# The second block's side tasks begin one in four slots instead of four in five

## The chip, the cores and the metric

The kernel runs on one core of one Trainium2 chip, as one program with one launch. The metric is device time in microseconds of one execution. Three executions of the kernel before took 2336.18 us in the median (2334.62 to 2336.28).

The engines are named as in the profile: PE is TensorE (matmuls; PEld its weight loads), DVE is VectorE, ACT is ScalarE, POOL is GpSimd, SP is SyncE, which issues the loads of the weights.

## The reference, cut to what matters

Everything is float32. A two-layer first block (attention, pooling, a Fourier mix; 256 tokens and 256 context tokens, width 2048) gives `x`, and a second block of one layer works on it. The second block's first half is what the change touches:

```
h = rmsnorm(x, norm1_g)
p = h @ w_in                                  # 2048 -> 4096 columns
u, v = split(gelu(p[:, :2048]))               # 1024 columns each
v = layernorm(v);  mixed = tril(ws) applied over 128-token chunks, per head, + bs
y_gm = u * mixed
g, xl = p[:, 2048:3072], p[:, 3072:]
xr = causal convolution of xl over 4 tokens
r, i = sigmoid(xr @ wa + ba), sigmoid(xr @ wx + bx)      # per head
a = exp(-8 * r * softplus(-lam)); b = sqrt(1 - a*a) * i * xr
y_lru = scan(h_t = a_t * h_{t-1} + b_t) * gelu(g)
x = x + concat(rmsnorm(y_gm), rmsnorm(y_lru)) @ w_out
```

After it come the feed-forward half (2048 to 2 x 6144 columns with a convolution of 3 tokens, then back to 2048) and a last rmsnorm.

## The kernel before, in words

**Matmuls.** Features lie on partitions, 128 at a time: `self.h[k]` is the k-th of 16 tiles. To keep float32 precision, each operand is split into a high part (rounded to the PE's format) and a low part (the rest), and each product is three matmuls: high x high, high x low, low x high (`mm3`, L203 to L205). Weights come from memory as 128 x 1024 blocks (`wraw`), are split by ACT (`whi`, L263) and DVE (`wlo`, L264) into one of three buffers each, and are used by 24 matmuls of 256 columns, or 12 of 512. A buffer is free again when its matmuls are done. The weight splits are written with high priority once the kernel's startup is over.

**The second block's projections.** `block2` (L1061) runs four projections of 1024 columns, 16 weight blocks each, which I call P1 to P4 by their order: P1 the recurrence's input (columns 3072 on), evacuated by `lru_front` (L1114); P2 `v`, evacuated by `evac_v` (L1172); P3 the recurrence's gate, evacuated by `lru_out` (L1159); P4 `u`, evacuated by `gm_out` (L1194), which also does the small matmuls that mix `v` (`gm_mix`, L1200). The last two of a projection's 16 blocks are one step, and the evacuations stand in that step. Then all that is waiting is run (`flush`), and the output projection follows, two times 1024 columns, over the order k = 8 to 15 (the recurrence's tiles) and then 0 to 7 (the gm tiles). Its evacuation is `resid2` (L1228).

**The side work.** What is neither a projection nor its evacuation is a task: a Python function put in a queue with `defer` while the program is written. The queue is served in order, first come first served. `spend` (L174) counts the time of the projections' matmuls by a formula of the kernel's own and calls `tick` once per 1.25 us of it. A tick is a slot. It goes on with tasks that have asked to pause for some slots (`yield n`), adds `start_rate` to a credit that is capped at 4, and begins a task for each whole credit while fewer than four are paused. `flush` ticks until queue and paused tasks are empty, without any matmul between. The tasks of P1 to P4, in the order in which they enter the queue:

- `block2_rstd` (L979; pauses 8, then 3 slots): the two norms' scales `r1`, `r12`, which `lru_front` needs
- `begin`: takes the tile for the two sums of squares, `sqm` and `sql`
- at the end of P1, eight `lru_conv` (L1119), then eight `lru_gates` (L1128; pause 2 slots) and eight `lru_scan` (L1152; a Sqrt on ACT, a product on POOL, the scan on DVE)
- at the end of P2, two `layernorm_v` (L1178)
- at the end of P3, eight `lru_gate` (L1165): the product with the gate, its square (`sum_sq`, L872, on ACT) and the sum of squares on POOL; then `norm_branch` for the recurrence (L1213; pauses 6 slots)
- at the end of P4, `norm_branch` for the gm tiles (pauses 0 slots)

`norm_branch` sums over features with a matmul by ones (`ssum`, L503), takes the power -0.5 on POOL (L497), broadcasts it by a matmul (`rbc`, L526), and for each of eight tiles makes the product `yn` (DVE, L1222), its high part (ACT, L263) and its low part (DVE, L264).

**What sets the order on an engine.** The program is written in one order, and the framework's scheduler then lays out each engine's instructions: of those that are ready it takes the one of highest priority, which is the one written first, except that the weight splits go ahead. An engine runs its own list strictly in that order. Short-lived tiles come from rings: `S` (L56) has seven tiles and holds `xl`, `gl`, `gu` (the evacuations), the squares `sqt`, `yn`, `rbn`, `res` and more. `C` (L53) has eight and holds `xr`, `vt` and `ym`.

The lines that make a slot's starts:

```
        self.start_acc = min(self.start_acc + self.start_rate, 4.0)
        while self.start_acc >= 1.0 and self.queue and len(self.active) < 4:
```

Of the kernel before, what the change touches and what calls it, by code (L numbers as in the profile page):

```python
# [32 lines left out]
class Kern:  # L33
# [1027 lines left out]
    def block2(self):  # L1061
        nc, a = self.nc, self.a
        w_in, w_out = a["w_in_2"][0], a["w_out_2"][0]
        ks = list(range(KT))
        hi = lambda k: self.h[k][0][:, 0:256]
        lo = lambda k: self.h[k][1][:, 0:256]
        self.xr, self.yl, self.ym = [None] * 8, [None] * 8, [None] * 8
        self.vt, self.yh, self.h3 = {}, {}, []

        later = lambda fn, *args: ([], partial(self.defer, fn, *args))  # L1070

        def begin():
            sqp = self.E("sqp")
            self.sqm, self.sql = sqp[:, 0:256], sqp[:, 256:512]

        steps = [([], self.flush), later(self.block2_rstd), later(begin), ([], partial(self.rate, 0.8))]
        steps += self.proj_fm(w_in, 3072, 1024, ks, hi, lo, NX, self.lru_front)
        steps += [later(self.lru_gates, i) for i in range(8)] + [later(self.lru_scan, i) for i in range(8)]
        steps += self.proj_tm(w_in, 1024, 1024, ks, hi, lo, 2, self.evac_v)
        steps += [later(self.layernorm_v, t) for t in range(2)]  # L1080
        steps += self.proj_fm(w_in, 2048, 1024, ks, hi, lo, NX, self.lru_out)
        steps.append(later(self.norm_branch, self.yl, "lru_out_g", 8))
        steps += self.proj_fm(w_in, 0, 1024, ks, hi, lo, NX, self.gm_out)
        steps += [later(self.norm_branch, self.ym, "gm_out_g", 0), ([], self.flush)]
        order = list(range(8, 16)) + list(range(8))

        def begin_out():
            self.sq2 = self.E("sq2")[:, 0:256]
            self.x2d = self.dr.tile([NX, D], F32, name="x2d")
        steps.append(([], begin_out))  # L1090

        def evac(g, b, ps):
            for j in range(2):
                self.resid2(g * 8 + b * 2 + j, ps[:, j * 256:(j + 1) * 256])
        for g in range(2):
            steps += self.proj_fm(w_out, g * 1024, 1024, order, lambda k: self.yh[k][0], lambda k: self.yh[k][1], NX,
                                  partial(evac, g))

        def end():
            yield 8  # L1100
            rb = self.rstd_tokens(self.sq2, 2, D)
            self.r3b = self.E("r3b", shape=(P, 256))
            nc.vector.tensor_copy(self.r3b, rb[:, :256])
        steps.append(later(end))
        return steps
# [305 lines left out]
```

## Time and profile before

| | us |
|---|---|
| median of three executions | 2336.18 |
| the profiled execution | 2334.31 |
| its span | 2332.5 |
| PE busy | 2254.2 |
| DVE busy | 1605.9 |
| ACT busy | 1007.1 |
| POOL busy | 205.9 |

Of the span, the second block's P1 to P4 take about 1190 to 1397 us and the output projection about 1397 to 1489 us. The feed-forward half follows to the end. Busy times of different engines overlap, so they don't add up to the span. An engine's idle time is put down to what ended it. A matmul's duration in a row is longer than the distance to the next one, because matmuls are pipelined: with 256 columns they start 0.12 us apart and show 0.28 us.

### The profile page before, as it was taken

Reading aid. Unit: us, or ns where it says so; the run is one execution under the profiler, and the core shown is the slowest. Engines: PE = TensorE matmul, PEld = TensorE weight load, DVE = VectorE, ACT = ScalarE, POOL = GpSimd, SP = SyncE. Lnnn points to the kernel's source line nnn. Section 1 sums busy time; section 2 is a strip of 40 time slices with the busy share of each in tenths; the row PEclk is TensorE's granted clock in tenths of the full one; section 3 lists DMA queues with packets and bytes.
Section 4 is the critical chain, followed back from the end, with each engine's and each line's share of the span. In section 5 each row is a group of like instructions: output and inputs, shape, how many; then the busy total and the mean of one; then the engine's idle time right before and its main releaser. Section 6 shows DMA issues by size and latency. Waiting matters only on the chain. (4 is left out here: it accounts for less than half of the span.)

```text
span 2332.5 us, 37418 instructions
## 1 busy us (share of the span) xinstructions
PE 2254.2 (97%) x14672; PEld 1977.0 (85%) x14672; DVE 1605.9 (69%) x2575; ACT 1007.1 (43%) x1511; POOL 205.9 (9%) x262
## 2 busy tenths in 40 slices
PE   7899999999999999999999999999999999999998
PEld 3567778777778878799998899999999999988886
DVE  3369988799987768655678776656676576564444
ACT  3133443223223554444446554544554455443433
POOL 1011011100112110100221111200000000000100
PEclk9999999999999999999999999999999999999999
DMA  9896545466866556655554555666566665765564
GB/s 316 288 310 209 154 125 152 127 209 209 277 216 212 173 170 208 192 152 183 171 169 156 173 164 167 195 192 186 183 182 183 185 184 182 220 205 189 185 188 142
DMA packets 202720, 447.88 MB, mean 192 GB/s; under 512 B 15848, under 2 KB 60288, under 8 KB 202544
## 3 DMA queue, kind: packets, MB, share of 16 engines
q1 hardware_dynamic: 193088, 428.93, 59.0%
q0 software_dynamic: 3888, 11.18, 1.4%
q10 hardware_dynamic: 5568, 5.40, 0.8%
q8 instruction: 115, 1.88, 0.3%
q14 instruction: 61, 0.50, 0.1%
HBM read 437.05 MB, written 8.39 MB: 191 GB/s over the span
## 5 line engine op out<-in xcount | busy, mean ns | idle before, releaser
L264 DVE TENSOR_TENSOR wlo<-wraw,whi 128x1024 fp32r<-128x1024 f32 x608 | 751.6, 1239 | 541.5 <-ACT whi L263 540.1
L263 ACT CAST whi<-wraw 128x1024 fp32r<-128x1024 f32 x608 | 636.0, 1049 | 925.6 <-PE acc L204 585.8
L203 PE MATMUL acc<-phi,whi 128*128 128x256 f32 (+1 forms) x1600 | 477.1, 298 | 0.9 <-DVE xT L830 0.8
L205 PE MATMUL acc<-phi,wlo 128*128 128x256 f32 (+1 forms) x1600 | 473.7, 296 | 3.5 <-DVE wlo L264 3.5
L204 PE MATMUL acc<-plo,whi 128*128 128x256 f32 (+1 forms) x1600 | 473.7, 296 | 0.0
L203 PE MATMUL acc<-h3t,whi 128*128 128x256 f32 x1536 | 435.2, 283 | 2.0 <-DVE xT L1233 2.0
L204 PE MATMUL acc<-h3t,whi 128*128 128x256 f32 x1536 | 434.8, 283 | 0.0
L205 PE MATMUL acc<-h3t,wlo 128*128 128x256 f32 x1536 | 434.7, 283 | 0.0
L328 DVE SCALAR_TENSOR_TENSOR acc<-wraw,silu_c,acc 128x512 f32<-128x512 f32 x420 | 297.5, 747 | 40.0 <-DMA wraw<-in_ada_w_dram 38.4
L203 PEld LDWEIGHTS acc<-phi,whi 128*128 128x128 f32 x1600 | 302.6, 189 | 13.6 <-issue 3.6
L205 PEld LDWEIGHTS acc<-phi,wlo 128*128 128x128 f32 x1600 | 302.5, 189 | 13.6 <-DVE wlo L264 4.3
L204 PEld LDWEIGHTS acc<-plo,whi 128*128 128x128 f32 x1600 | 302.8, 189 | 9.1 <-issue 0.5
L203 PEld LDWEIGHTS acc<-h3t,whi 128*128 128x128 f32 x1536 | 294.8, 192 | 2.7 <-DVE xT L1233 2.7
L205 PEld LDWEIGHTS acc<-h3t,wlo 128*128 128x128 f32 x1536 | 294.8, 192 | 0.1
L204 PEld LDWEIGHTS acc<-h3t,whi 128*128 128x128 f32 x1536 | 294.8, 192 | 0.0
L203 PE MATMUL acc<-hhi,whi 128*128 128x512 f32 x384 | 159.2, 415 | 1.1 <-ACT whi L263 1.1
L204 PE MATMUL acc<-hlo,whi 128*128 128x512 f32 x384 | 153.4, 400 | 0.0
L205 PE MATMUL acc<-hhi,wlo 128*128 128x512 f32 x384 | 152.0, 398 | 0.2 <-DVE wlo L264 0.2
L204 PE MATMUL acc<-wlo,act 128*128 128x512 f32 x384 | 151.7, 395 | 0.0
L205 PE MATMUL acc<-whi,act 128*128 128x512 f32 x384 | 151.7, 395 | 0.0
L203 PE MATMUL acc<-whi,act 128*128 128x512 f32 x384 | 151.7, 395 | 0.0
L203 PEld LDWEIGHTS acc<-hhi,whi 128*128 128x128 f32 x384 | 72.9, 190 | 22.2 <-issue 4.6
(350 smaller groups left out, 2790.2 us busy)
## 6 DMA issues: line engine op xcount, KB each, us to landing
wraw<-in_w_in_dram SPq DMA_DIRECT2D x216, 512.0 KB, 3.9
wraw<-in_ffn_w_up_dram SPq DMA_DIRECT2D x192, 512.0 KB, 3.6
wraw<-in_ada_w_dram SPq DMA_DIRECT2D x128, 512.0 KB, 4.4
wraw<-in_w_out_dram SPq DMA_DIRECT2D x104, 512.0 KB, 4.2
wraw<-in_ffn_w_down_dram SPq DMA_DIRECT2D x96, 512.0 KB, 3.8
apage<-in_ada_w_dram SPq DMA_DIRECT2D x128, 256.0 KB, 6.0
xd<-xT SPq DMA_DIRECT2D x16, 256.0 KB, 4.7
xT<-xd POOLq DMA_DIRECT2D x16, 256.0 KB, 5.6
```

The costliest lines, as they stand in the source:

```text
L203: mm(out, lhi, rhi, start=start, stop=False)
L204: mm(out, lhi, rlo, start=False, stop=False)
L205: mm(out, llo, rhi, start=False, stop=stop)
L263: self.nc.scalar.copy(hi, src)
L264: self.nc.vector.tensor_tensor(lo, src, f(hi), ALU.subtract)
L328: nc.vector.scalar_tensor_tensor(acc[m], x, cm, acc[m], ALU.mult, ALU.add)
```

## The change

One number: the credit that a slot adds while the second block's projections run is 0.25 instead of 0.8. The next change of the rate, to 0.3 at the beginning of the feed-forward half, stays.

```
-        steps = [([], self.flush), later(self.block2_rstd), later(begin), ([], partial(self.rate, 0.8))]
+        steps = [([], self.flush), later(self.block2_rstd), later(begin), ([], partial(self.rate, 0.25))]
```

## Rows read from the trace of the kernel before

**Rows 1.** The page's first part: busy us, share of the span, instructions.
```profile
PE 2254.2 (97%) x14672; PEld 1977.0 (85%) x14672; DVE 1605.9 (69%) x2575; ACT 1007.1 (43%) x1511; POOL 205.9 (9%) x262
```

**Rows 2.** Stretches P2 and P4: length, busy time by engine, granted clock, DMA share, GB/s.
```profile
1242.60:1299.50 56.90, 53.02 (x227) 41.54 (x226) 56.71 (x78) 42.49 (x61) 15.35 (x15) 1.00 0.44 140
...
1346.00:1397.30 51.30, 50.84 (x429) 50.43 (x428) 35.88 (x57) 27.75 (x43) 10.83 (x11) 1.00 0.52 167
```

**Rows 3.** Waits, 1205 to 1500 us: who for whom, total us, times, longest.
```profile
PE acc L204 <- DVE wlo L264: 3.8, 4, 2.9
...
PE acc L205 <- DVE wlo L264: 1.0, 1, 1.0
```

**Rows 4.** Timeline of DVE: start us, duration, instruction, idle before it.
```profile
1418.06 0.42 DVE L1232 TENSOR_TENSOR res<-xT,rbp 128x256 f32<-128x256 f32 x1
...
1443.16 0.42 DVE L1232 TENSOR_TENSOR res<-xT,rbp 128x256 f32<-128x256 f32 x1
```

**Rows 5.** Timeline of PE, the small matmuls of the norms and P4's end.
```profile
1210.40 0.61 PE L985 MATMUL s<-ones,sq 128*128 128x1 f32 x4 [2.65 <-POOL sq L880]
...
1361.39 0.50 PE L503 MATMUL ssum<-ones,sqp 128*128 128x1 f32 x4
...
1363.26 0.71 PE L526 MATMUL rbc<-bcw,ones 128*128 128x128 f32 x4 [0.43 <-DVE bcw L525]
...
1397.37 0.36 PE L203 MATMUL acc<-phi,whi 128*128 128x256 f32 x1
...
1406.32 0.61 PE L503 MATMUL ssum<-ones,sqp 128*128 128x1 f32 x4 [1.24 <-POOL sqp L880]
...
1408.38 0.68 PE L526 MATMUL rbc<-bcw,ones 128*128 128x128 f32 x4 [0.29 <-DVE bcw L525]
```

**Rows 6.** Timeline of POOL behind P4: the last additions, the power.
```profile
1403.62 0.74 POOL L880 TENSOR_TENSOR sqp<-sqp,sqt 128x256 f32<-128x256 f32 x1 [2.13 <-ACT sqt L879]
1404.88 1.38 POOL L880 TENSOR_TENSOR sqp<-sqp,sqt 128x256 f32<-128x256 f32 x1 [0.51 <-ACT sqt L879]
1407.20 0.71 POOL L497 TENSOR_TENSOR rs_col<-rs_col,nhalf 128x2 f32<-128x2 f32 x1 [0.94 <-DVE rs_col L496]
```

**Rows 7.** Timeline of ACT and DVE in the two norms and between.
```profile
1364.93 0.80 ACT L263 CAST phi<-yn 128x256 fp32r<-128x256 f32 x2 [0.55 <-DVE yn L1222]
...
1401.47 1.23 DVE L264 TENSOR_TENSOR wlo<-wraw,whi 128x1024 fp32r<-128x1024 f32 x1 [0.46 <-ACT whi L263]
...
1409.19 0.36 ACT L1219 COPY rbn<-rbc 128x256 f32<-128x256 f32 x1
```

**Rows 8.** Groups by line of DVE, 1390 to 1421 us: busy, mean ns, idle before.
```profile
L1222 DVE SCALAR_TENSOR_TENSOR yn<-ym,cols,rbn 128x256 f32<-128x256 f32 x8 | 3.5, 482 | 0.0
...
L264 DVE TENSOR_TENSOR plo<-yn,phi 128x256 fp32r<-128x256 f32 x8 | 3.0, 421 | 0.0
```

**Rows 9.** Stretches of 2 us in P1; PE's granted clock is third from the end.
```profile
1212.00:1214.00 2.00, 1.41 (x10) 1.25 (x9) 1.18 (x4) 0.40 (x1) 0.71 (x1) 0.71 0.17 64
1214.00:1216.00 2.00, 2.00 (x11) 2.00 (x11) 1.56 (x6) 0.00 (x0) 0.00 (x1) 0.50 0.28 74
```

**Rows 10.** Groups by line of ACT, 1240 to 1305 us: busy, mean ns, idle before.
```profile
L263 ACT CAST whi<-wraw 128x1024 fp32r<-128x1024 f32 x18 | 18.4, 1042 | 3.9 <-PE acc L205 3.4 <-ACT xr L1123 0.5
L1141 ACT ACTIVATE lt<-lz,hba 128x256 f32<-128x256 f32 x16 | 6.9, 473 | 0.0
L1155 ACT ACT_TABLE_LOAD x5 | 6.4, 1283 | 0.6 <-DVE xT L1148 0.6
L1144 ACT ACTIVATE xT<-lt,m2sp 128x256 f32<-128x256 f32 x8 | 4.8, 600 | 0.0
...
L1155 ACT ACTIVATE xT<-xT 128x256 f32<-128x256 f32 x8 | 3.2, 416 | 3.5 <-DVE xT L1148 3.5
```

**Rows 11.** Timeline of ACT: a table load and the Sqrt behind it.
```profile
1262.89 1.28 ACT L1155 ACT_TABLE_LOAD   x1
1264.19 0.42 ACT L1155 ACTIVATE xT<-xT 128x256 f32<-128x256 f32 x1
```

## The prediction

> **What bounds the kernel now.** I read the page's first part first: TensorE (PE) is busy 97% of the span [rows 1]. So a change pays or costs only where it takes away or adds idle time of PE. The change touches one part, the second block's four input projections P1 to P4 (1190 to 1397 us), so I then took the stretches P2 and P4 apart [rows 2]. In P2 VectorE (DVE) is busy 56.7 of 56.9 us and PE 53.0; in P4 DVE has 15 us to spare and PE is busy 50.8 of 51.3. The waits of 1205 to 1500 us say what PE lost in P2 and early P3: 3.8 + 1.0 us for a low half from DVE [rows 3]. That is the recurrence's burst of tasks in front of the weight splits. The side work after P2 costs PE next to nothing, because it is finished in time.
>
> **The change, part by part.** It removes and adds no instruction. It moves the place at which a task's instructions are written, so I counted slots. A projection spends 16 x 8 x 0.32 = 40.96 us of its own reckoning, 32.8 slots of 1.25, so P1 to P4 end at slots 32.8, 65.5, 98.3 and 131.1. Credit is capped at 4 and is full when P1's evacuations come at slot 30, so the first four convolutions start at slots 30 and 31 at either rate. From there:
> - before (0.8): gates at 39 to 47, scans 47 to 55, layernorm 66, output gates of the recurrence (`lru_gate`) 95 to 100, its norm 102 + 6 = 108. All are written before P4 ends; only the gm norm (133) is not.
> - after (0.25): convolutions 4 to 7 at 34 to 46, gates 52 to 80, scans 82 to 110, layernorm 114 and 118, `lru_gate` 0 and 1 at 122 and 126, number 2 at 130 and numbers 3 to 7 at 134 to 150 behind P4's last matmul, then the gm norm (159) and only behind it the recurrence's norm (160).
>
> The output projection takes the recurrence's eight tiles first. So what stood in the middle of P4 now stands between P4 and the next matmul.
>
> *How far the build pulls instructions forward.* It does: the product `res` of the output evacuation runs at 1418.06, 24 us ahead of the evacuation that it is written in, and past weight splits that are written before it. But only one does: its neighbour, whose inputs were ready as early, waits until 1443.16 although DVE had idle time all along [rows 4]. I read this as tiles of the S ring being given out in written order. Products without an S tile can move up (the eight `lru_gate` products, scans, layernorm); the squares 2 to 7, which write an S tile, cannot pass the four `gu` tiles of P4's end, nor the recurrence's norm the eight tiles of the gm norm.
>
> *Term 1, the tail.* On the clock of the run before, the output projection's first matmul starts at 1397.4 [rows 5]. After the change it needs, in a row:
> - the gm sum of squares. GpSimd (POOL) ends it at 1404.88 + 1.38 = 1406.3 [rows 6]. A split of 1.23 us stands on DVE on the way [rows 7]; it is one that PE's progress releases, so with PE still it falls away: 1405.3.
> - five squares of the recurrence, added on POOL behind it. One takes 0.74, or 1.38 with a split on DVE beside it [rows 6]; DVE has little beside these, so I take 0.8: + 4.0 = 1409.3.
> - power, broadcast and copy of the gm norm: from 1407.20 to 1409.19 + 0.36 [rows 6, 7], 2.35 us: 1411.7. The recurrence's own power and broadcast run beside the next step.
> - eight products and eight low halves of the gm tiles on DVE: 8 x (0.482 + 0.421) = 7.2 by the means [rows 8], about 6.1 where they overlap at start to start; I take 6.6: 1418.3.
> - the first product of the recurrence and its high half on ScalarE (ACT), 0.48 + 0.41: 1419.2.
>
> PE stands 1419.2 - 1397.4 = 21.8 us. Three waits of the two norms, 0.43 + 1.24 + 0.29, go, and so do some 1.7 us that their four groups of small matmuls take in line (2.5 us by their durations, less overlap) [rows 5]: net +18.1. From both sides: if the gm power goes ahead of the five additions, 4 us less; if nothing is pulled up, the six products stand in the tail too, 2.5 us more, and with the additions at 1.38 another 2.9.
>
> *Term 2, the clock.* After PE's stall of 2.65 us at 1210.40 the granted clock was 0.71 and then 0.50, the 1.2 GHz level, for two windows of 2 us [rows 5, 9]: 2 x 0.29 + 2 x 0.5 = 1.6 us lost. A stall of 20 us should bring it too; I take 1.7, bounds 0 and 3.4 (one more such stretch).
>
> *Term 3, P2 and P3.* The load spreads: a gate every 4 slots, which is 6.4 us of PE with its own four matmuls. DVE's burst goes, and with it up to 4.8 us of waits [rows 3]. But a scan's Sqrt has no S tile and is ready before the next gate's Tanh, so ACT would change table for each. Per gate ACT then does two splits (2.08), three Tanh (0.95 + 0.60), a Sqrt (0.42) and two loads (2.57): 6.6 us in 6.4 [rows 10], before any wait for DVE. The gain needs ACT to keep up and the row says that it is just full. I take 0, bounds -4.8 and +8 (1.4 us of waiting for DVE's reciprocal before each of eight Sqrt, less some 3.4 us by which the splits run ahead of PE).
>
> The Trainium skill, page "ScalarE: Activation LUTs" (section "What ACT_TABLE_LOAD costs"), puts a change of set at 1283 ns and as much again for a drain, some 2.66 us, and asks to batch calls by set, which speaks against this change. This trace agrees on the load (1.28) but shows no drain: the load starts at 1262.89 and the Sqrt at 1264.19 [rows 11]. By the page's price ACT would need 9.3 us per gate, an estimate: 8 x 2.9 - 3.4 = +20 on top of the tail, near 2376. I keep to the row.
>
> *Term 4, the start of P1.* `block2_rstd` is written two slots later (12, not 10). Its matmul at 1210.40 already stands further down than slot 10, where its sums were thought due, so the 2.65 us remain [rows 5]. I take 0; if it slips by all of two slots, the wait and its clock dip go: -4.3.
>
> Sum: 18.1 + 1.7 + 0 + 0 = +19.8. The profiled execution took 2334.31 (span 2332.5), 1.9 below the median 2336.18, and would take 2354.1; on the median that is 2356.0.
>
> **The rivals.**
> - Only the norm is exposed. If S tiles are not given in order, the squares run during P4 and the recurrence's sum is ready; then PE waits from its sums matmul to the first high half, 1361.39 to 1364.93 + 0.41 = 3.95 us, less 0.43 and 0.8, plus the clock 1.7: +4.4, 2340.6. For it: eight products can move up. Against it: the lone `res` [rows 4].
> - ACT is the bound in P2 and P3: the tail as above and +8 from the tables, 2364. For it: ACT's 6.6 in 6.4 [rows 10]. Against: some Sqrt may fall together, as now.
> - Faster. The whole tail, the small norm matmuls too, is put into P4, where DVE has 15 us free [rows 2], and the even load takes away P2's waits: -4.8, 2331.4. It decides itself at one place: whether the recurrence's sums matmul stands ahead of P4's last matmul on PE. Against it: it is written behind, and PE has ready work all through P4.
> - The change does not do what it says: the order on the engines follows readiness so far that the slots hardly matter, 2336. Against: the flush puts instructions behind P4 whatever their readiness.
>
> **How the numbers follow.** Forecast 0.66, exposed norm 0.14, ACT bound 0.11, faster 0.06, no effect 0.03. A measurement of this kernel tells 0.2%, 4.7 us, from no change at best. Range 2340 to 2366: the low end takes in the exposed norm, which lies at 0.19% and is counted half as same and half as slower; the high end the ACT case. The forecast's own range is 2349 to 2362. Faster 0.06; same 0.03 + 0.07 = 0.10; slower 0.66 + 0.11 + 0.07 = 0.84.
>
> **What would show it.** One idle of PE of 16 to 25 us after P4's last `gmm`, ended by `phi` or `plo` of the recurrence; before it on DVE eight `yn<-ym` ahead of the first `yn<-xT`; the additions `sqp` of both branches back to back on POOL; a granted clock of 0.5 behind it. In P2 the five waits for a low half mostly gone, or replaced by waits for ACT with up to sixteen table loads. I am wrong if `yn<-xT` still runs in the middle of P4, or if PE's idle behind P4 is under 8 us.

## The result, and the profile after

The kernel after the change took 2350.06 us (median, 2345.48 to 2355.64), the kernel before beside it 2335.4: ratio 1.0069, 95% interval 1.0055 to 1.0083, so +16 us. (The two medians differ by 14.7 us. A timed difference, here and below, is the ratio on record less one, times the median of the kernel before.) The forecast was 2356.0, by the same mechanism with a sum of +19.8. The profiled execution took 2351.13 us, span 2349.1 (before 2334.31 and 2332.5).

Busy times by engine, of the kernel after (engine, us, share, instructions): nothing was added but four table loads on ACT (1515 instructions where [rows 1] has 1511); PE runs the same 14672 instructions, and the span grew by 16.6 us.

```profile
PE 2257.7 (96%) x14672; PEld 1982.3 (84%) x14672; DVE 1605.6 (68%) x2575; ACT 1013.9 (43%) x1515; POOL 210.0 (9%) x262
```

Stretches P2, P4, and a third between P4's last matmul and the output projection's first (length, busy time and count of PE, its weight loads, DVE, ACT and POOL, then granted clock, DMA share, GB/s):

```profile
1242.60:1296.00 53.40, 53.19 (x245) 43.35 (x244) 43.33 (x61) 35.21 (x46) 7.66 (x6) 1.00 0.51 159
1343.50:1395.10 51.60, 51.60 (x440) 51.60 (x439) 30.53 (x42) 24.69 (x31) 3.90 (x4) 1.00 0.56 180
1395.10:1415.30 20.20, 4.67 (x20) 3.77 (x18) 12.45 (x29) 10.07 (x26) 9.46 (x12) 0.63 0.15 53
```

In P2, DVE was busy 56.7 of 56.9 us before [rows 2] and is now busy 43.3 of 53.4: the burst is spread. The third stretch did not exist before; there the output projection followed at 1397.37 [rows 5]. Its 4.67 us of PE are, but for 0.3, the two norms' small matmuls.

PE's timeline at the same places (start, duration, instruction, idle before it and who ended it):

```profile
1209.82 1.01 PE L985 MATMUL s<-ones,sq 128*128 128x1 f32 x4 [2.65 <-POOL sq L880]
...
1394.28 1.05 PE L1204 MATMUL gmm<-gw,vt 128*128 128x128 f32 x8
1402.43 1.01 PE L503 MATMUL ssum<-ones,sqp 128*128 128x1 f32 x4 [7.11 <-POOL sqp L880]
1405.45 1.19 PE L526 MATMUL rbc<-bcw,ones 128*128 128x128 f32 x4 [2.01 <-DVE bcw L525]
1406.88 1.01 PE L503 MATMUL ssum<-ones,sqp 128*128 128x1 f32 x4 [0.24 <-POOL sqp L880]
1409.35 1.19 PE L526 MATMUL rbc<-bcw,ones 128*128 128x128 f32 x4 [1.46 <-DVE bcw L525]
1415.27 0.79 PE L203 MATMUL acc<-phi,whi 128*128 128x256 f32 x2 [4.72 <-ACT phi L263]
```

The first row is Term 4: 2.65 us of waiting, as in [rows 5]. The others are the tail. Both norms stand there one behind the other, and the last wait is for a high half (`phi`) of the recurrence, as forecast.

POOL in the tail. The gm power (1403.82) went ahead of the last three recurrence additions, where [rows 6] has gm additions and one power only:

```profile
1400.85 3.01 POOL L880 TENSOR_TENSOR sqp<-sqp,sqt 128x256 f32<-128x256 f32 x4 [0.93 <-ACT sqt L879]
1403.82 0.71 POOL L497 TENSOR_TENSOR rs_col<-rs_col,nhalf 128x2 f32<-128x2 f32 x1
1404.49 2.34 POOL L880 TENSOR_TENSOR sqp<-sqp,sqt 128x256 f32<-128x256 f32 x3
1408.17 0.71 POOL L497 TENSOR_TENSOR rs_col<-rs_col,nhalf 128x2 f32<-128x2 f32 x1 [1.34 <-DVE rs_col L496]
```

DVE in the tail. Its row for the recurrence's norm at 1408.92 stands ahead of the first gm product, and all eight gm products stand ahead of the first recurrence product at 1414.30:

```profile
1408.92 0.29 DVE L525 TENSOR_SCALAR bcw<-ident,rs_col 128x128 f32<-128x128 f32 x1 [0.83 <-POOL rs_col L497]
1409.12 1.27 DVE L1222 SCALAR_TENSOR_TENSOR yn<-ym,cols,rbn 128x256 f32<-128x256 f32 x3
...
1413.51 0.87 DVE L1222 SCALAR_TENSOR_TENSOR yn<-ym,cols,rbn 128x256 f32<-128x256 f32 x2
1414.30 0.48 DVE L1222 SCALAR_TENSOR_TENSOR yn<-xT,cols,rbn 128x256 f32<-128x256 f32 x1
```

The clock (same columns as the stretches; granted clock is third from the end). It fell about 5 us after P4's end to 0.50, the 1.2 GHz level, stayed there, and came back only within 1420 to 1422, 5 to 6 us into the output projection. In 2 us at half clock PE ran 11 matmuls, later 19:

```profile
1398.00:1400.00 2.00, 0.00 (x0) 0.00 (x0) 1.58 (x3) 0.63 (x1) 1.84 (x3) 1.00 0.69 264
1400.00:1402.00 2.00, 0.00 (x0) 0.00 (x0) 0.53 (x2) 1.71 (x6) 1.07 (x2) 0.56 0.60 213
...
1418.00:1420.00 2.00, 2.00 (x11) 2.00 (x11) 2.00 (x6) 1.20 (x3) 0.00 (x0) 0.50 0.00 0
1420.00:1422.00 2.00, 2.00 (x16) 2.00 (x15) 1.09 (x4) 1.27 (x2) 0.00 (x0) 0.82 0.00 0
1422.00:1424.00 2.00, 2.00 (x19) 2.00 (x18) 1.38 (x2) 0.45 (x2) 0.00 (x0) 1.00 0.00 0
```

Where the time went, from the starts of four PE rows in each profile: the first sums matmul of P1 (line 985), P2's first matmul of 512 columns, the first `gmm` of P4, the output projection's first matmul, and its first residual transposition (`x2t`). Work before line 985 is the same in all kernels and varies from execution to execution (last section), so only stretches behind it are compared. The last column is the difference that the timed runs show (ratio less one, by the median of the kernel before beside it). All in us:

| kernel | P1 | P2 to first gmm | first gmm to output proj. | output proj. to x2t | sum | sum against before | timed difference |
|---|---|---|---|---|---|---|---|
| before | 32.27 | 146.93 | 7.77 | 49.87 | 236.84 | | |
| after | 32.90 | 144.61 | 27.94 | 49.47 | 254.92 | +18.1 | +16.1 |
| e1_catch_up | 32.91 | 145.93 | 7.95 | 51.83 | 238.62 | +1.8 | 0.0 |
| e2_tail_alone | 32.34 | 144.96 | 24.03 | 48.12 | 249.45 | +12.6 | +12.8 |
| e3_norm_first | 32.96 | 144.59 | 25.58 | 49.04 | 252.17 | +15.3 | +14.7 |
| e4_squares_ahead | 31.28 | 144.57 | 17.88 | 48.49 | 242.22 | +5.4 | +6.3 |
| e5_rate_04 | 31.51 | 144.31 | 7.74 | 49.86 | 233.42 | -3.4 | -3.7 |
| e6_rate_03 | 31.46 | 141.51 | 26.11 | 54.62 | 253.70 | +16.9 | +11.0 |
| e7_warm | 31.47 | 144.60 | 28.96 | 47.06 | 252.09 | +15.3 | +16.3 |
| e8_no_sqrt_table | 31.27 | 143.86 | 27.93 | 48.97 | 252.03 | +15.2 | +17.7 |
| e9_03_catch_up | 31.27 | 142.83 | 7.77 | 49.90 | 231.77 | -5.1 | -3.5 |
| e10_rate_05 | 33.04 | 142.01 | 7.77 | 51.41 | 234.23 | -2.6 | -1.9 |

Read the row of the kernel after against that of before. Behind P4 it is +20.2. From P2 to the first gmm it is -2.3, of which 0.6 are waits for a low half and the rest is the recurrence's norm, which no longer stands in P4. In the output projection it is -0.4, which is -2.8 of the gm norm no longer in it and +2.4 of half clock (e7_warm, whose output projection ran at 1.00 throughout and without the norm, needs 47.06). P1 is +0.6, with a clock dip that held longer. Sum +18.1.

Two rows hold a clock dip that has nothing to do with a tail. In e1_catch_up and e10_rate_05 the granted clock falls to 0.50 in the output projection, behind PE's wait for the gm sum (1.84 and 1.24 us), and that column is 1.5 to 2.0 us above the kernel before. The kernel before, e5_rate_04 and e9_03_catch_up wait 1.2 to 1.3 us at the same place and stay at 1.00. So the +1.8 of e1_catch_up is about this dip and not the spread. A stretch of 2 us in the dip of e10_rate_05:

```profile
1405.00:1407.00 2.00, 2.00 (x11) 2.00 (x11) 2.00 (x5) 0.88 (x3) 0.00 (x0) 0.50 0.17 35
```

### The profile page after: what moved, and what is told of

The parts are those of the page before. It is cut to its first block, busy times and chain, and to the rows that moved or that the text cites. A ratio compares the mean times of both kernels' runs of the same rounds, so it can differ in the third digit from the quotient of the medians.

```text
span 2349.1 us, 37425 instructions
## 1 busy us (share of the span) xinstructions
PE 2257.7 (96%) x14672; PEld 1982.3 (84%) x14672; DVE 1605.6 (68%) x2575; ACT 1013.9 (43%) x1515; POOL 210.0 (9%) x262
## 5 line engine op out<-in xcount | busy, mean ns | idle before, releaser
L205 PEld LDWEIGHTS acc<-phi,wlo 128*128 128x128 f32 x1600 | 305.0, 191 | 17.8 <-DVE wlo L264 8.5
```

Of the source, the lines that this page charges most:

```text
L205: mm(out, llo, rhi, start=False, stop=stop)
```

## The experiments

Theory: what costs time is only the work written behind P4's last matmul, in a chain that the order of the S tiles and of POOL and DVE sets, with half clock behind it. Rivals: the spread itself costs (a fuller ACT, table loads); the time goes down evenly with the rate.

**e1_catch_up**: the slow rate for P1 to P3, the old one from there.

```diff
         steps += self.proj_fm(w_in, 2048, 1024, ks, hi, lo, NX, self.lru_out)
+        steps.append(([], partial(self.rate, 0.8)))
         steps.append(later(self.norm_branch, self.yl, "lru_out_g", 8))
```

> The rate stays 0.25 through P1, P2 and P3 and is set back to 0.8 behind P3's last matmul, so that the rest of the queue begins during P4. Theory (the loss is the side work that lands between P4 and the output projection): P1 to P3 as in the changed kernel, no idle behind P4, about 1 us below the kernel before, 2334. Rival (the even spread costs time in P2 and P3, by table loads on ACT and by DVE): stays near the changed kernel, 2345 or more.

Measured 2333.79 on 2333.72, ratio 1.000 (0.999 to 1.001). The whole loss is gone with the tail. The recurrence's norm stands in P4 again, without a wait for its sums:

```profile
1380.07 0.50 PE L503 MATMUL ssum<-ones,sqp 128*128 128x1 f32 x4
...
1382.28 0.71 PE L526 MATMUL rbc<-bcw,ones 128*128 128x128 f32 x4 [0.18 <-DVE bcw L525]
...
1410.38 0.61 PE L503 MATMUL ssum<-ones,sqp 128*128 128x1 f32 x4 [1.84 <-POOL sqp L880]
```

What follows: the spread of convolutions, gates and scans over P1 to P3 costs nothing that these runs can tell (the interval is 2.3 us either way). That ACT is the bound there, at a cost of 8 us, is ruled out.

**e2_tail_alone**: the counterpart, the old rate for P1 and P2 and a very slow one from P3, so that only the tail is made.

```diff
+        steps.append(([], partial(self.rate, 0.1)))
         steps += self.proj_fm(w_in, 2048, 1024, ks, hi, lo, NX, self.lru_out)
```

(and 0.8 in place of 0.25 at the block's start.)

> The rate is 0.8 as before through P1 and P2, and 0.1 from the beginning of P3: P2 runs as in the kernel before, and six of the eight output gates and the recurrence's norm fall behind P4. Theory: an idle of PE behind P4 of about 20 us and a half clock behind it, 2353. Rival (loss in P2 and P3): back to the kernel before, 2336.

Measured 2346.35, ratio 1.0055 (1.0041 to 1.0069): +12.8. The tail alone makes most of the loss, but less than expected. Rows of PE, ACT and DVE tell why: the first wait is 9.43 us, four of the recurrence's squares run behind P4 (they write `sqt` from `xT`), and its first products come ahead of the gm products.

```profile
1399.19 1.01 PE L503 MATMUL ssum<-ones,sqp 128*128 128x1 f32 x4 [9.43 <-POOL sqp L880]
1394.69 1.32 ACT L879 ACTIVATE sqt<-xT 128x256 f32<-128x256 f32 x4
1404.71 1.27 DVE L1223 SCALAR_TENSOR_TENSOR yn<-xT,cols,rbn 128x256 f32<-128x256 f32 x3
```

The expectation had taken the change's own tail, and missed in two places of the slot count. At 0.1 four output gates are written behind P4, not six; in the kernel after six squares run there. And the recurrence's norm is written ahead of the gm norm, so this tail is like that of the next experiment: 16.3 us longer than before in the table, not 20.2.

**e3_norm_first**: the change with the recurrence's norm not put off by six slots, so that it is written ahead of the gm norm.

```diff
-        yield 6 if k0 else 0
+        yield 0
```

> The changed kernel with one number more: the recurrence's norm no longer pauses six slots, and so is written ahead of the gm norm. The eight gm products leave the way to the output projection. Theory: the idle behind P4 ends some 4 to 5 us earlier (near 1411 instead of 1415.3 on the changed kernel's clock), 2345 to 2346. Rival (the order of the two norms is nothing, the sums set the idle): 2350.

Measured 2347.39, ratio 1.0063 (1.0049 to 1.0076): +14.7, against +16.1 of the change. The eight gm products no longer stand ahead of the recurrence's first (the last row, of DVE), and yet only some 2 us came back (25.58 against 27.94 in the table), where 4 to 5 were expected. PE's rows, and that one:

```profile
1407.73 1.02 PE L503 MATMUL ssum<-ones,sqp 128*128 128x1 f32 x4 [10.99 <-POOL sqp L880]
1410.20 1.19 PE L526 MATMUL rbc<-bcw,ones 128*128 128x128 f32 x4 [1.46 <-DVE bcw L525]
1411.19 0.85 PE L503 MATMUL ssum<-ones,sqp 128*128 128x1 f32 x4
1413.48 1.19 PE L526 MATMUL rbc<-bcw,ones 128*128 128x128 f32 x4 [1.45 <-DVE bcw L525]
1414.33 1.20 PE L203 MATMUL acc<-phi,whi 128*128 128x256 f32 x4
1413.25 1.27 DVE L1222 SCALAR_TENSOR_TENSOR yn<-xT,cols,rbn 128x256 f32<-128x256 f32 x3
```

The sums now wait until 1407.73 for POOL to add the squares of both branches, and PE takes both norms' small matmuls before the first projection matmul, which itself waits for nothing. Taking one link out of a chain gave back only what the next link left.

**e4_squares_ahead**: as e3, with the recurrence's squares in a B tile instead of an S tile, so that they need not pass the gm tiles of P4 in the ring.

```diff
-        self.sum_sq(self.sql, y, i == 0)
+        if i == 0:
+            nc.scalar.activation(self.sql, y, AF.Square)
+        else:
+            sq = self.B("sqg")
+            nc.scalar.activation(sq[:, :256], y, AF.Square)
+            nc.gpsimd.tensor_tensor(self.sql, self.sql, sq[:, :256], ALU.add)
```

> As e3, and the squares of the output gates take their tiles from the idle B ring instead of S. Theory (squares 2 to 7 stood behind the gu tiles because S tiles are given out in written order): all eight squares and their additions run in P4, the sum of the recurrence is ready before P4 ends, and PE waits for its norm and the gm sum only: start near 1405, idle 9 to 11 us, 2340. Rival (the squares stand behind P4 because they are written there, whatever the ring): as e3, 2345.

Measured 2338.01, ratio 1.0027 (1.0016 to 1.0038): +6.3. The recurrence's sums matmul follows P4's last `gmm` without a wait, and the broadcast 5.9 us later:

```profile
1391.91 0.50 PE L503 MATMUL ssum<-ones,sqp 128*128 128x1 f32 x4
1397.82 1.19 PE L526 MATMUL rbc<-bcw,ones 128*128 128x128 f32 x4 [5.41 <-DVE bcw L525]
...
1401.96 1.20 PE L203 MATMUL acc<-phi,whi 128*128 128x256 f32 x4
```

ACT's timeline, first of the kernel after, where two of the recurrence's squares run at 1348.83 and 1350.08 and the other six behind P4, then of e4, where all eight run by 1350.6:

```profile
1350.08 0.41 ACT L879 ACTIVATE sqt<-xT 128x256 f32<-128x256 f32 x1
...
1396.82 0.40 ACT L879 ACTIVATE sqt<-xT 128x256 f32<-128x256 f32 x1
...
1400.95 1.62 ACT L879 ACTIVATE sqt<-xT 128x256 f32<-128x256 f32 x5
```

```profile
1345.59 0.40 ACT L1171 ACTIVATE sqp<-xT 128x256 f32<-128x256 f32 x1
1346.84 1.64 ACT L1174 ACTIVATE sqg<-xT 128x256 f32<-128x256 f32 x5
...
1349.66 0.96 ACT L1174 ACTIVATE sqg<-xT 128x256 f32<-128x256 f32 x2
```

What follows: the ring of S tiles is what held the squares back, as the prediction read it off the lone `res`. That alone is worth 7.7 us (25.58 less 17.88 in the table) of the 17.8 that e3 has in excess of before (25.58 less 7.77). The 10.1 us that are left lie within the 9 to 11 expected. DVE's timeline shows two places in them that no run takes apart. The first step of the recurrence's scale (`rs_col`) runs at 1395.40, 3.0 us after its sums, behind two weight splits and the last `gu`. And the recurrence's first product, at 1400.88, follows the gm norm's `bcw` at 1400.68.

**e5_rate_04, e6_rate_03, e10_rate_05**: the change with 0.4, 0.3 and 0.5 in place of 0.25.

> The changed kernel with a rate of 0.4 in place of 0.25 for the whole block. Theory (what costs time is only that the two norms' sums and products are written behind P4's last matmul): at 0.4 the recurrence's products and its norm are written before P4's last column block, so no wait is left behind P4 and the time is that of the kernel before within 0.1%, 2333 to 2336 us. Rival (the cost grows with the spreading itself, through a fuller ScalarE and VectorE in P2 to P4): a third to a half of the 16 us remains, 2339 to 2343 us.

> The changed kernel with a rate of 0.3. Theory: the recurrence's eighth products come right before P4's last column block and its norm is written behind the gm norm, so the squares are mostly out of the way, but both norms' sums, powers, broadcasts and the first eight gm products still stand between P4's last matmul and the output projection: TensorE idle 14 to 17 us there (20.2 in the changed kernel), 2344 to 2348 us. Rival (the cost goes down evenly with the rate from 0.25 to 0.4): 2344.5 us too, but with an idle stretch of 7 to 10 us, which the trace tells apart.

> A rate of 0.5 for the whole block. Theory (above some rate nothing is left behind P4, and the lower the rate is above that point, the less VectorE work falls together in P2): no idle stretch, between 0.4 (3.7 to 4.1 us below before) and 0.8, so 2329 to 2332 us. Rival (the gain at 0.4 is one order that happens to fit): 2332.5 to 2334 us, with P2 and P3 within 0.5 us of the kernel before.

Measured: 0.5 gives 2330.35, ratio 0.9992 (0.9980 to 1.0005); 0.4 gives 2328.93, ratio 0.9984 (0.9975 to 0.9992); 0.3 gives 2344.4, ratio 1.0047 (1.0035 to 1.0059). So the loss is a step between 0.4 and 0.3, not a slope: at 0.4 there is no idle stretch behind P4, at 0.3 PE stands 18 us. That is 1 us over the 14 to 17 expected and far from the 7 to 10 of the even slope. The 5 us by which 0.25 is slower than 0.3 are, in the table, 1.8 in the tail and 3.1 ahead of it. 0.3 in one view:

```profile
1389.00:1407.25 18.25, 4.20 (x18) 3.64 (x17) 11.33 (x29) 8.48 (x21) 6.01 (x7) 0.56 0.18 58
```

And 0.4 beats the kernel before by some 3.7 us, more than expected. The waits of PE from 1205 to 1500 us (who for whom, total, times, longest), of e5_rate_04, show 1.7 us for a low half where [rows 3] has 3.8 and 1.0:

```profile
PE acc L205 <- DVE wlo L264: 1.7, 2, 1.2
```

At 0.5 the time is the one expected, but its interval takes in no gain at all. The theory behind it, that the gain grows as the pace falls towards the step, does not come out of the traces: PE's waits for a low half in the same view are 0.7 us at 0.5, 1.7 at 0.4 and at 0.3, and 4.3 at 0.25.

**e7_warm**: the change with fourteen matmuls that nobody reads behind P4, meant to hold the clock.

```diff
         def begin_out():
+            fill = self.accs(1)[0]
+            for i in range(14):
+                nc.tensor.matmul(fill, self.ones, self.wab["a", i % 2].rearrange("p h j -> p (h j)"),
+                                 start=i == 0, stop=i == 13)
```

> The changed kernel with fourteen matmuls of 512 columns that nobody reads (ones by a gate weight, into a free accumulator) written behind P4's last matmul. They run while TensorE would stand and wait for the norms' sums. Theory (the half clock after the idle stretch costs its own term, 2.7 us in the trace): the granted clock stays at 1.00 through the stretch or comes back within it, the output projection restarts at full clock, and the time falls by 2 to 4 us against the changed kernel, to 2346 to 2348 us on its 2350. Rival: the fillers run at half clock themselves and hold up the two norms' small matmuls, no gain or 1 to 3 us more, 2350 to 2353 us.

Measured 2350.23, ratio 1.0070 (1.0058 to 1.0082): no gain that can be told, so the expected time was missed. The two stretches (tail, output projection up to x2t) and POOL's timeline show what happened:

```profile
1395.10:1416.20 21.10, 16.50 (x46) 8.18 (x44) 12.34 (x29) 10.01 (x26) 9.47 (x12) 0.84 0.15 50
1416.20:1463.30 47.10, 47.08 (x397) 47.05 (x398) 27.53 (x44) 20.51 (x28) 1.91 (x2) 1.00 0.48 157
```

```profile
1400.79 4.62 POOL L880 TENSOR_TENSOR sqp<-sqp,sqt 128x256 f32<-128x256 f32 x6 [0.93 <-ACT sqt L879]
1405.36 0.71 POOL L497 TENSOR_TENSOR rs_col<-rs_col,nhalf 128x2 f32<-128x2 f32 x1
```

The clock fell to 0.50 within the tail all the same (0.84 over the stretch), but it was back before the output projection, which ran at 1.00 from its first matmul and took 47.06 us, 2.4 less than in the kernel after. But the build then put the gm power behind two more additions (six in this row, four in the kernel after), 1.5 us later, and the tail grew by 1.0. Net -1.4 in the profile, which these runs can't tell from nothing; the time of a change without that side effect stays open.

**e8_no_sqrt_table**: the change with a Tanh in place of the scan's square root. It leaves the root out, so that ACT needs no table for it.

```diff
-        nc.scalar.activation(th, th, AF.Sqrt, scale=-1.0)
+        nc.scalar.activation(th, th, AF.Tanh, scale=-1.0)
```

> The changed kernel with a Tanh in place of the scan's square root (the root is left out, so ScalarE needs no square-root table there). It takes away the table loads that the spread scans bring between P2 and P3. Theory (VectorE's load sets P2's and P3's waits for the low halves, and the loads are hidden): P2 and P3 keep 3 to 4.3 us of waits for wlo, time within 1 us of the changed kernel, 2349 to 2351 us. Rival (the loads on ScalarE set those waits): P3's waits go, 2 to 4 us less, 2346 to 2348 us.

Measured 2350.21, ratio 1.0076 (1.0063 to 1.0089): unchanged. Between 1240 and 1345 us ACT loads a table once, where the kernel after does so 14 times (the kernel before ten), and PE's waits for the low half are still there, 3.6 us against 4.3:

```profile
PE acc L205 <- DVE wlo L264: 3.6, 5, 1.6
```

What follows: thirteen loads of 1.28 us are hidden but for some 0.75 us from P2 to the first gmm (144.61 less 143.86), too little to see in the time.

**e9_03_catch_up**: e1 with 0.3 in place of 0.25, to keep the gain of the even load without the tail.

> The rate of 0.3 up to the end of P3 and 0.8 from there. Rows so far: from the first block-2 sum to the first transposition of the residual, P2 and P3 together took 5.4 us less than before at 0.3, 2.6 less at 0.4 and 1.0 less at 0.25 with the rate of 0.8 behind P3. Theory (the gain in P2 and P3 and the loss behind P4 are two separate things): no idle stretch behind P4, P2 and P3 keep at least 2.5 us of their gain, 2328 to 2331 us on a kernel before of 2333. Rival (what is put off in P2 and P3 comes back in P4 once it is hurried there): 2332 to 2335 us.

Measured 2330.22 on 2332.11, ratio 0.9985 (0.9975 to 0.9996); the medians alone differ by 1.9 us. No stretch behind P4 (7.77 in the table), P2 to the first gmm 4.1 us shorter than before. So gain and loss are two separate things and the gain can be kept. This version and e5_rate_04 are the two that beat both kernels; between them these runs can't choose.

## Why the prediction was right, and where its sizes were off

- **Term 1, the tail: right in mechanism, 1.6 us too long.** Predicted idle 21.8, measured 20.2, ended by `phi` of the recurrence as said. Its links: the gm sum was ready 7.3 us after P4's last matmul (forecast 7.9). The power then did go ahead of three of the five additions, the case that the prediction had priced at -4 as a bound; it gained nothing, since the link "the recurrence's own power and broadcast run beside the next step" failed: on DVE its `bcw` at 1408.92 stands ahead of the first gm product, which had its factor from 1407.05 (ACT's copy, 1406.68 + 0.37). So the first gm product came 14.0 us after P4's end (forecast 14.3, from 1397.4 to 1411.7): two errors that cancel, which is luck. From there to the first recurrence product 5.2 us, not 6.6: of eight low halves two came behind it.
- **What goes in return: forecast 1.96 of waits and 1.7 of matmul groups, 3.7 together; measured 1.7 in P4 and 2.8 in the output projection, 4.5.** The groups cost about their whole durations in line, 2.5 us, where I had taken 0.8 off for overlap.
- **Term 2, the clock: forecast 1.7, measured 2.4.** I sized it by a stall of 2.65 us whose dip lasted two stretches of 2 us [rows 9]; after 20 us the half clock held until 5 to 6 us into the restart. The profile of e7_warm shows that the term is real.
- **Term 3, P2 and P3: forecast 0, measured -0.6.** The waits for the low half went from P2 and early P3 (before 3.8 + 1.0, [rows 3]) into P3 (4.3 in six, all but 0.2 of it there). The price per load, 1.28 without a drain, holds; fourteen loads came where up to sixteen were feared, and e8_no_sqrt_table shows them hidden. The Trainium skill's price of a change of set with its drain (page "ScalarE: Activation LUTs", section "What ACT_TABLE_LOAD costs") would have given 2376 by the prediction's estimate; the measured time is 2350. This trace agrees on the load and not on the drain: two loads of the kernel after, with a Sqrt between them, start at 1275.93 and 1277.66, only 1.73 us apart.
- **Term 4, the start of P1: 0, as forecast.** The 2.65 us remain to the digit.
- **The S ring**, read from one instruction that was pulled up and one that was not [rows 4], carried the whole forecast. e4_squares_ahead confirms it: with another tile the squares run early.
- The rivals: "only the norm is exposed" is near what e4_squares_ahead makes (+6.3 against the +4.4 worked out); "ACT is the bound" falls by e1_catch_up and e8_no_sqrt_table; "faster" needed a rate at which the recurrence's sums matmul stands ahead of P4's last matmul, and e5_rate_04 and e9_03_catch_up are just that, 3.5 to 3.7 us faster where the rival had said 4.8. That alone is not enough: e1_catch_up has it too and gains nothing, with 4.3 us of waits for a low half.

The sum of the terms as the profile measures them is +18.1 at x2t and +16.6 over the span; the timed runs say +16.1, between 12.8 and 19.4. The rest is within what executions differ by.

## What to carry to other kernels

A pace for side work has a deadline: the last matmul behind which the flush puts whatever is left. Count in slots whether the last task is written before it; up to there a slower pace can even gain by an even load (0.4 here, though the gain does not grow evenly as the pace falls), beyond it the cost comes as a step (0.3), since the whole chain of sums, power, broadcast and products then stands in front of TensorE. When only a few steps miss the deadline, look for the shared tile ring or in-order queue that holds them, and change that before the pace: a different tile for the squares gave back 7.7 us.

## What the hardware showed beyond that

- Executions of the same instructions differ before the change's place: P1's first sums matmul starts between 1204.45 us (e2_tail_alone) and 1211.20 (e3_norm_first), and P1 itself takes 31.3 us where the granted clock stays at 1.00 (e4_squares_ahead, e8_no_sqrt_table, e9_03_catch_up) and up to 33.0 us where it dips. No kernel was profiled twice, so how far apart two profiles of one kernel lie is not shown; stretches, not absolute times, were comparable.
- In the profile of e6_rate_03 PE runs 77 matmuls in 10 us behind the tail, at a granted clock of 1.00, where the kernel after runs 86 in a like stretch. It lasts until about 1460 us and explains most of the 5.9 us by which its row in the table stands above its timed difference. No other profile shows it between 1180 us and the end, and its cause is open. First e6_rate_03, then the kernel after:

```profile
1420.00:1430.00 10.00, 10.00 (x77) 10.00 (x76) 4.08 (x4) 3.14 (x3) 0.00 (x0) 1.00 0.54 181
```

```profile
1430.00:1440.00 10.00, 10.00 (x86) 10.00 (x86) 4.75 (x4) 3.53 (x4) 0.00 (x0) 1.00 0.62 197
```
